# Where a hybrid decoder layer spends its spare wide products: a new deal over the recurrence's chain, the memory's norm and the attention

## The chip, the cores and the metric

The kernel is one program on one core of a Trainium2 chip. Its time is device microseconds (us) of that core, the median of several runs. The engines of the core are TensorE (PE in the profile, PEld for its weight loads), VectorE (DVE), ScalarE (ACT), GpSimd (POOL) and SyncE (SP), which issues nearly all DMA transfers here.

## The reference

One layer of a causal decoder trunk, 1024 tokens of width 1024, in float32. Three branches read the same normalised input `h` through one combined projection `w_in`:

```python
h = rms_norm(x, norm_mix_pre)
z_pool, z_q, z_rwkv, z_gate = split(h @ w_in)     # 512, 512, 3328, 3 x 1024 columns

y_pool = pool_branch(z_pool, ...) @ w_proj_pool   # causal means over 2, 4, 8, 16 tokens, 4 groups

mem_n = rms_norm(mem, mem_norm)                   # 256 memory tokens
k, v  = split(mem_n @ w_mem_kv)                   # 4 heads x 128
y_mem = softmax(q k^T / sqrt(128)) v @ w_proj_mem

zr = z_rwkv + (token_shift(z_rwkv) - z_rwkv) * mu_shift
# RWKV-7: 16 heads of 64, for each token t:
#   sa    = state @ (-kk_t)
#   state = state * w_t + sa (kk_t a_t)^T + v_t k_t^T ;  y_t = state @ r_t
y_rwkv = (groupnorm(y) + bonus) * g @ w_proj_rwkv

gates  = sigmoid(z_gate + gate_b)                 # 3 gates
x = x + rms_norm((gates0*y_pool + gates1*y_rwkv + gates2*y_mem) @ w_o)
x = x + rms_norm(convffn(rms_norm(x)))
```

## The kernel before, in words

**Wide products in triples.** Each float32 operand of a wide product is split into a coarse part and a rest (`hh`, `hl` for the input, `whi`, `wlo` for weights), and `mm3` issues three products 128x512 into one bank: coarse by coarse, coarse by rest, rest by coarse. Three such products are called a triple. The weights come from memory as `wraw` (loads of two k-slices), ScalarE makes `whi` by a cast, GpSimd or VectorE makes `wlo`.

**The recurrence** runs over 16 chunks of 64 tokens. In `chain`, each chunk visits TensorE three times: `pr` (the state and the decayed keys give a right-hand side, copied to `Rs`), `pu` (the inverted triangular matrix, `nt`, times `Rs`, copied to `hv`), and `ph` with `py` (the next state and the output). That makes 48 visits, each waiting for a copy of the one before. The chunks' matrices were written to memory earlier (`d_ar`, `d_nt`, ...) and are loaded by SP two chunks at a time; `nt` lies in the tile that the rows call `pair`. Outputs are normalised with a product `pvar` and stored to `d_y`.

**The filler.** While a visit waits, TensorE is given wide products that nobody needs yet: the projection's blocks of the pool (4), the queries (4) and the gates (24), in the list `fill`. A block is two halves of 512 tokens by eight k-slices, so 16 triples, 512 triples in all. `fill_steps` issues one triple at a time, and when a half is complete, `spilled` evacuates it (ScalarE to `st`, SP to `d_zp`, `d_zq` or `d_zg`). `fill_to(n)` issues triples until n have been issued, and returns the last one. Visit v calls `fill_to(fills(v))` and orders its own first product behind the last triple. A scheduler then orders each engine's instructions by their data and by such hints (`later`).

**The memory and the attention.** Behind the chain, `fill_to(416)` returns `covered`. SP loads the memory (`mraw` from `memT`, eight parts, into room that the chain leaves), ScalarE squares the parts (`msq`, `msqp`), VectorE adds them, and the product `pmm` with a matrix of ones sums over the channels; it is ordered behind `covered`. `mrs` is the reciprocal root of the sum, VectorE multiplies the parts by it, and `mh`, `ml` are the coarse part and the rest. Eight blocks of `w_kv` follow (eight triples each, products of 128x256): four of keys (`kh`, `kl`), four of values, which are transposed (`pvt`, function `turned`) as `vh`, `vl`. Weights of the first two come as `wraw`, of the other six as `kvr` (512 KB, two rooms). Then four heads of attention, each in two halves: scores `psco`, softmax `prb`, transposes `ptr`. Behind each head the products of the pooling and some of the blocks that are left in `fill` (`in_block`) are written.

Of the kernel before, what the change touches and what calls it, by code (L numbers as in the profile page):

```python
# [44 lines left out]
def trunk_kernel(ctx: ExitStack, tc: tile.TileContext, xT, memT, pvec, w_in, w_kv, w_upd, w_upg,  # L45
# [129 lines left out]
    last_mm = [None]  # L175
# [46 lines left out]
    def later(i, ins, plain=False):  # L222

        tc.add_manual_dep(i if plain else i.ins, ins.name, nosync, reason="order")
# [79 lines left out]
    def hrhs(t0):  # L304
        return lambda k: (hh[:, k, t0:t0 + 512], hl[:, k, t0:t0 + 512])
# [35 lines left out]
    def spilled(dst, bias=None):  # L341
        def evac(t0, ps):
            st = wp.tile([P, 512], F32, name="st", tag="st", bufs=3)
            if bias is None:
                spills.append(A.copy(st, ps).ins)
            else:
                A.activation(st, ps, AF.Identity, bias=bias)
            SP.dma_start(dst[:, t0:t0 + 512], st)
        return evac
# [123 lines left out]
    def rwkv_group(g, kv):  # L473
# [183 lines left out]
        if g == 3:  # L657
            w_queue[0] = A
            fill_to(256, solve)
# [186 lines left out]
    fill = [(j, spilled(d_zp[j])) for j in range(4)] + [(4 + j, spilled(d_zq[j])) for j in range(4)]  # L846
    fill += [(34 + j, spilled(d_zg[j], col("gate_b", j))) for j in range(24)]
    filled = []

    def fill_steps(j, evac, behind):  # L850

        ws = load_w(w_in[j], KC, c=1)
        for t0, _ in HALVES:
            ps = psg.tile([P, 512], F32, name="psg", tag="g1")
            rhs = hrhs(t0)
            for k in range(KC):
                m = mm3(ps, ws[k], rhs(k), k == 0, k == KC - 1)
                if k == 0 and behind is not None:
                    later(m, behind)
                filled.append(last_mm[0])  # L860
                if k == KC - 1:
                    evac(t0, ps)
                yield

    current = [iter(())]

    def fill_to(n, behind=None):

        while len(filled) < n:
            if next(current[0], 0) == 0:  # L870
                current[0] = fill_steps(*fill.pop(0), behind)
        return filled[n - 1]

    first_kv = start()
# [4 lines left out]
    hi_on_act[0] = True  # L879
    for g in range(4):  # L880
        kv = rwkv_group(g, kv)
    chain(lambda v: 262 + 138 * v // 47)
    covered = fill_to(416)
    w_queue[0] = SP
    spare[0] = None
    rw_ctx.close()
# [16 lines left out]
    with tc.tile_pool(name="km", bufs=1) as km:  # L903
# [12 lines left out]
        m = PE.matmul(pmm[:, :256], ones, total, start=True, stop=True)  # L916
# [41 lines left out]
        turned(*waiting.pop())  # L958

        lo_on_dve[0] = False  # L960


    pz_ctx = ExitStack()
# [47 lines left out]
    for hd in range(4):  # L1011
        for t0, _ in HALVES:
            s = slice(t0, t0 + 512)
            q = as_.tile([P, 512], F32, name="q", tag="q", bufs=2)
            SP.dma_start(q, d_zq[hd][:, s])
            qh = as_.tile([P, 512], FR, name="qh", tag="qh")
            ql = as_.tile([P, 512], FR, name="ql", tag="ql")
            split(q, qh, ql, V)
            po = pss.tile([P, 512], F32, name="po", tag="s")
            for u in range(2):  # L1020
                ps = psg.tile([P, 2, 256], F32, name="psco", tag="g0")
                for tt in range(2):
                    ts_ = slice((2 * u + tt) * P, (2 * u + tt + 1) * P)
                    mm3(ps[:, tt], (qh[:, ts_], ql[:, ts_]), (kh[:, hd], kl[:, hd]), True, True)
                mx = as_.tile([P, 32], F32, name="mxs", tag="mxs", bufs=2)
                V.reduce_max(mx[:, 0:2], ps, axis=AX.X)
                V.tensor_scalar(mx[:, 2:4], mx[:, 0:2], -SC, None, op0=ALU.mult)
                pr = as_.tile([P, 2, 256], F32, name="prb", tag="prb", bufs=2)
                for tt in range(2):
                    act(pr[:, tt], ps[:, tt], AF.Exp, bias=mx[:, 2 + tt:3 + tt], scale=SC,  # L1030
                        accum_out=mx[:, 4 + tt:5 + tt])
                V.reciprocal(mx[:, 6:8], mx[:, 4:6])
                V.tensor_tensor(pr, pr, mx[:, 6:8].unsqueeze(2).broadcast_to([P, 2, 256]), op=ALU.mult)
                pt = (psc if u else psk).tile([P, 2, 2, P], F32, name="ptr", tag="c" if u else "k")
                for tt in range(2):
                    for m in range(2):
                        PE.transpose(pt[:, m, tt], pr[:, tt, m * P:(m + 1) * P], ident)
                pth = as_.tile([P, 2, 256], FR, name="pth", tag="pth", bufs=2)
                ptl = as_.tile([P, 2, 256], FR, name="ptl", tag="ptl")
                split(pt.rearrange("p m t s -> p m (t s)"), pth, ptl, V)  # L1040
                for m in range(2):
                    mm3(po[:, u * 256:(u + 1) * 256], (vh[:, hd, m], vl[:, hd, m]), (pth[:, m], ptl[:, m]),
                        m == 0, m == 1)
            split(po, oh[hd][:, s], ol[hd][:, s], V)
        pool_products(hd)
        if hd < 2:
            pool_sums(hd + 2)
        for j, ev in fill[hd + min(hd, 2):hd + min(hd, 2) + (2 if hd < 2 else 1)]:
            in_block(j, ev, 1)

    as_ctx.close()
# [794 lines left out]
```

## Time and profile before

| | |
|---|---|
| median of 3 runs | 1961.81 us (1959.63 to 1962.59) |
| profiled execution | 1961.22 us, span 1959.5 us |
| mean granted TensorE clock | 0.997 |
| TensorE busy | 1912.1 us, 98% of the span |
| VectorE, ScalarE, GpSimd busy | 1361.5, 1044.3, 791.9 us |
| from 680 to 696 us (the chain's first two visits): TensorE busy | 13.23 of 16 us |
| from 696 to 889 us (the rest of the chain) | 192.88 of 193 us |
| from 889 to 909 us (to the ones product) | 17.94 of 20 us |
| from 909 to 942 us (norm, keys, values) | 33.00 of 33 us, at a mean clock of 0.96 |
| from 942 to 1030 us (attention) | 84.49 of 88 us |

Times are those of one profiled execution, counted from the span's start. A row of the timeline gives start, duration, engine, line, operation, result and operands, shapes, and how many equal ones it stands for; in brackets, how long the engine had stood idle before it and who released it. `L916` is line 916 of the kernel before. An engine that is busy all the time can still be slow: the granted clock says at what share of its full speed TensorE ran.

### The profile page before, as it was taken

What the parts mean: (1) busy time and instruction counts of PE and PEld (TensorE: products, weight loads), DVE (VectorE), ACT (ScalarE), POOL (GpSimd) and SP (SyncE); (2) the same over time, 40 slices, a digit from 0 to 9 for tenths busy, and PEclk for the clock granted to TensorE, in tenths of its full rate; (3) what the DMA queues carried; (4) which work ended last, traced back from release to release, by engine and by line L of the source; (5) the groups of instructions that cost most, each with busy time, mean ns of one, the idle gap of its engine ahead of it and who ended that gap; (6) DMA issues with size and microseconds to landing.
All of it is one profiled execution on the core that took longest, in us unless ns stands there. A gap on an engine that the chain in (4) does not pass through costs nothing.

```text
span 1959.5 us, 33751 instructions
## 1 busy us (share of the span) xinstructions
PE 1912.1 (98%) x12204; PEld 1543.9 (79%) x12204; DVE 1361.5 (69%) x2022; ACT 1044.3 (53%) x2158; POOL 791.9 (40%) x867
## 2 busy tenths in 40 slices
PE   8999999999999999999999999999999999999997
PEld 6777777777777777777888888888888888888886
DVE  8677567677677435546884443689798888877798
ACT  7685385385384244445665244546554545454544
POOL 4422221321321211111223365565599888822441
PEclk9999999999999999999999999999999999999999
DMA  4325235225239668966318343644322222289775
GB/s 162 129 71 177 96 86 175 90 86 175 94 107 279 190 207 279 300 215 212 108 59 274 123 144 111 225 150 133 122 76 87 81 87 76 97 241 227 172 182 146
DMA packets 269639, 296.26 MB, mean 151 GB/s; under 512 B 18336, under 2 KB 219168, under 8 KB 266400
## 3 DMA queue, kind: packets, MB, share of 16 engines
q1 hardware_dynamic: 248480, 271.56, 43.2%
q0 software_dynamic: 11856, 14.16, 4.4%
q10 hardware_dynamic: 9136, 8.39, 1.4%
q8 instruction: 96, 1.57, 0.3%
q14 instruction: 71, 0.58, 0.1%
HBM read 207.00 MB, written 87.03 MB: 150 GB/s over the span
## 4 chain that ended last, share of the span: by engine, by line
PE 77%; DVE 8%; DMA 6%; ACT 4%; issue 3%; POOL 1%; SPq 0%; ACTq 0%; POOLq 0%; DVEq 0%
PE psg L180 14%; PE psg L182 14%; PE psg L181 14%; PE psf L182 5%; PE psf L180 5%; PE psf L181 5%; PE psd L181 3%; PE psd L182 3%; PE psd L180 3%; PE py L770 2%; DMA wraw<-in_w_in 1%; PE ps L605 1%; DVE tb L651 1%; DVE tb L653 1%; DMA d_bv<-kv 1%
## 5 line engine op out<-in xcount | busy, mean ns | idle before, releaser
L139 POOL TENSOR_TENSOR wlo<-wraw,whi 128x256 fp32r<-128x256 f32 x464 | 410.7, 897 | 833.8 <-ACT whi L132 772.7
L180 PE MATMUL psg<-hh,whi 128*128 128x512 f32 x928 | 380.1, 410 | 12.2 <-ACT whi L132 5.9
L182 PE MATMUL psg<-hh,wlo 128*128 128x512 f32 x928 | 368.0, 397 | 2.7 <-POOL wlo L139 2.2
L181 PE MATMUL psg<-hl,whi 128*128 128x512 f32 x928 | 367.8, 396 | 0.7 <-DVE hl L266 0.6
L132 ACT CAST whi<-wraw 128x256 fp32r<-128x256 f32 x472 | 181.2, 402 | 236.2 <-PE psg L181 99.1
L180 PEld LDWEIGHTS psg<-hh,whi 128*128 128x128 f32 x928 | 175.0, 189 | 60.1 <-ACT whi L132 11.2
L182 PEld LDWEIGHTS psg<-hh,wlo 128*128 128x128 f32 x928 | 175.0, 189 | 44.8 <-POOL wlo L139 7.2
L181 PEld LDWEIGHTS psg<-hl,whi 128*128 128x128 f32 x928 | 175.3, 189 | 40.5 <-issue 4.5
L1172 POOL TENSOR_TENSOR wt<-a,wt 128x256 fp32r<-128x256 f32 x136 | 155.6, 1168 | 35.1 <-ACT wt L1171 35.1
L181 PE MATMUL psd<-f,u 128*128 128x512 f32 x292 | 113.9, 390 | 0.2 <-DVE f L1588 0.2
L180 PE MATMUL psd<-f,u 128*128 128x512 f32 x292 | 113.2, 391 | 0.8 <-ACT f L1584 0.8
L182 PE MATMUL psd<-f,u 128*128 128x512 f32 x292 | 113.7, 389 | 0.0
L182 PE MATMUL psf<-h2h,wt 128*128 128x512 f32 x272 | 105.9, 389 | 0.0
L181 PE MATMUL psf<-h2l,wt 128*128 128x512 f32 x272 | 105.8, 389 | 0.0
L180 PE MATMUL psf<-h2h,wt 128*128 128x512 f32 x272 | 105.8, 389 | 0.0
L1186 DVE SCALAR_TENSOR_TENSOR d<-z,pv,d 128x1023 f32<-128x1023 f32 x68 | 101.2, 1491 | 2.1
L1172 POOL TENSOR_TENSOR wt<-s,wt 128x256 fp32r<-128x256 f32 x68 | 80.0, 1197 | 3.8 <-ACT wt L1171 2.6
L180 PE MATMUL psf<-t,wt 128*128 128x512 f32 x204 | 79.4, 389 | 0.0
L181 PE MATMUL psf<-t,wt 128*128 128x512 f32 x204 | 79.4, 389 | 0.0
L182 PE MATMUL psf<-t,wt 128*128 128x512 f32 x204 | 79.4, 389 | 0.0
L1184 ACT ACTIVATE d<-z,pv 128x1024 f32<-128x1024 f32 x34 | 42.4, 1246 | 65.3 <-DVE z L1266 49.8
L1171 ACT CAST wt<-a 128x256 fp32r<-128x256 f32 x136 | 50.6, 404 | 41.3 <-POOL wt L1172 25.9
(432 smaller groups left out, 4565.7 us busy)
## 6 DMA issues: line engine op xcount, KB each, us to landing
wraw<-in_w_in SPq DMA_DIRECT2D x176, 128.0 KB, 2.3
a<-in_w_fup SPq DMA_DIRECT2D x128, 128.0 KB, 2.3
d_ar<-AR SPq DMA_DIRECT2D x24, 512.0 KB, 3.7
d_zg<-st SPq DMA_DIRECT2D x48, 256.0 KB, 3.7
ring<-d_ar SPq DMA_DIRECT2D x8, 1536.0 KB, 10.5
wraw<-in_w_fup SPq DMA_DIRECT2D x80, 128.0 KB, 2.4
fraw<-d_f SPq DMA_DIRECT2D x33, 256.0 KB, 4.2
d_rb<-RB SPq DMA_DIRECT2D x16, 512.0 KB, 3.9
```

The lines of the kernel that those rows point to most:

```text
L132: i = A.copy(hi, src)
L139: (V if lo_on_dve[0] else G).tensor_tensor(lo, src, hi.bitcast(F32), op=ALU.subtract)
L180: first = PE.matmul(ps, wh, xh, start=start, stop=False)
L181: PE.matmul(ps, wh, xl, start=False, stop=False)
L182: last_mm[0] = PE.matmul(ps, wl, xh, start=False, stop=stop).ins
L605: PE.matmul(ps[:, c], BK[i][up, c0 + c], AR[up, i, 1:3, t], start=True, stop=True)
L651: V.tensor_tensor(tm, X[:, s + 1:, s:s + 1].broadcast_to([P, n, m]), S[:, s:s + 1, 0:m].broadcast_to([P, n, m]), op=ALU.mult)
L770: m = PE.matmul(out_, l, r, **kw)
L1171: A.copy(w[0][:, us], src[u])
L1172: low = eng.tensor_tensor(w[1][:, us], src[u], w[0][:, us].bitcast(F32), op=ALU.subtract)
L1184: A.activation(d, z, AF.Identity, scale=col("cw2", j), bias=col("cb", j))
L1186: V.scalar_tensor_tensor(d[:, n:], z[:, :T - n], col(cw, j), d[:, n:], op0=ALU.mult, op1=ALU.add)
```

## The change

It moves products; it adds none and takes none away.

- The rule that says how many triples are issued by visit v becomes `279 + 121*(v-1)//46` from the second visit on (it was `262 + 138*v//47`); the first visit keeps 262 and the last 400. So 17 triples stand between the first and the second visit, where there were 12.
- `covered`, behind which `pmm` is ordered, is the 424th triple (the end of a half block), where it was the 416th, the end of a block.
- Behind the last `turned`, half a block more (`fill_to(432, ...)`) is issued, ordered behind the values' last product.
- The five blocks left are written behind the heads as 1, 2, 1, 1; it was six, as 2, 2, 1, 1.
- So that a half block may have a hint of its own, `fill_steps` reads it from `tied[0]` when a half begins, instead of taking it when the block begins.

```diff
+    tied = [None]
-    def fill_steps(j, evac, behind):
+    def fill_steps(j, evac):
...
-                if k == 0 and behind is not None:
-                    later(m, behind)
+                if k == 0 and tied[0] is not None:
+                    later(m, tied[0])
...
     def fill_to(n, behind=None):
 
+        tied[0] = behind
         while len(filled) < n:
             if next(current[0], 0) == 0:
-                current[0] = fill_steps(*fill.pop(0), behind)
+                current[0] = fill_steps(*fill.pop(0))
         return filled[n - 1]
...
-    chain(lambda v: 262 + 138 * v // 47)
-    covered = fill_to(416)
+    chain(lambda v: 279 + 121 * (v - 1) // 46 if v else 262)
+    covered = fill_to(424)
...
         turned(*waiting.pop())
 
         lo_on_dve[0] = False
+        fill_to(432, last_mm[0])
...
-        for j, ev in fill[hd + min(hd, 2):hd + min(hd, 2) + (2 if hd < 2 else 1)]:
+        for j, ev in fill[hd + (hd > 1):hd + 1 + (hd > 0)]:
             in_block(j, ev, 1)
```

Where the products stand on TensorE is seen from the order of its instructions. First the chain's second visit, `pu`, before:

```order
L180 MATMUL psg_6746<-hh_146,whi_6723 128x512
L181 MATMUL psg_6746<-hl_147,whi_6723 128x512
L182 MATMUL psg_6746<-hh_146,wlo_6724 128x512
L770 MATMUL pu_6601<-Rs_6520,pair_6519 64x64 x16
L180 MATMUL psg_6746<-hh_146,whi_6729 128x512
```

and now:

```order
L180 MATMUL psg_6663<-hh_146,whi_6652 128x512
L181 MATMUL psg_6663<-hl_147,whi_6652 128x512
L182 MATMUL psg_6663<-hh_146,wlo_6653 128x512
L180 MATMUL psg_6663<-hh_146,whi_6658 128x512
L181 MATMUL psg_6663<-hl_147,whi_6658 128x512
L182 MATMUL psg_6663<-hh_146,wlo_6659 128x512
L770 MATMUL pu_6601<-Rs_6520,pair_6519 64x64 x16
L180 MATMUL psg_6663<-hh_146,whi_6658 128x512
```

Between the first visit and `pu` there are 51 wide products now, 36 before: `pu` comes five triples later in the row. From there to the last visit, the stretches between visits have 121 triples instead of 126, mostly three each in both, with 17 stretches of two now.

Next TensorE at the memory's ones product `pmm` (`msq` are the summed squares), before:

```order
L180 MATMUL psg_9848<-hh_146,whi_9815 128x512
L916 MATMUL pmm_9144<-msq_9145,ones_90 128x256
L181 MATMUL psg_9848<-hl_147,whi_9815 128x512
L182 MATMUL psg_9848<-hh_146,wlo_9816 128x512
L180 MATMUL psg_9900<-hh_146,whi_9877 128x512
L181 MATMUL psg_9900<-hl_147,whi_9877 128x512
```

and now:

```order
L181 MATMUL psg_9132<-hl_147,whi_9127 128x512
L182 MATMUL psg_9132<-hh_146,wlo_9128 128x512
L919 MATMUL pmm_9196<-msq_9197,ones_90 128x256
L180 MATMUL psg_9274<-mh_9224,whi_9251 128x256
L181 MATMUL psg_9274<-ml_9225,whi_9251 128x256
L182 MATMUL psg_9274<-mh_9224,wlo_9252 128x256
```

Ahead of `pmm`, behind the chain's last `pvar`, stand 46 wide products now, 68 before. Behind it the products of the first key block (`mh`, `ml`) follow at once; before there were ten wide products, and 29 more among the keys and values. None is left there now: from the last visit to the values' end, 72 wide products instead of 123.

Last, TensorE at the end of the values, where `pvt` are the transposes, before:

```order
L181 MATMUL psg_9553<-ml_9173,whi_9549 128x256
L182 MATMUL psg_9553<-mh_9172,wlo_9550 128x256
L943 MATMUL pvt_9578<-ident_92,vt_9533 128x128 x2
L180 MATMUL psg_9928<-hh_146,whi_9877 128x512
L181 MATMUL psg_9928<-hl_147,whi_9877 128x512
L182 MATMUL psg_9928<-hh_146,wlo_9878 128x512
L180 MATMUL psg_9928<-hh_146,whi_9883 128x512
L181 MATMUL psg_9928<-hl_147,whi_9883 128x512
L943 MATMUL pvt_9585<-ident_92,vt_9583 128x128 x2
```

and now:

```order
L181 MATMUL psg_9605<-ml_9225,whi_9601 128x256
L182 MATMUL psg_9605<-mh_9224,wlo_9602 128x256
L946 MATMUL pvt_9630<-ident_92,vt_9585 128x128 x2
L180 MATMUL psg_9642<-hh_146,whi_9109 128x512
L181 MATMUL psg_9642<-hl_147,whi_9109 128x512
L182 MATMUL psg_9642<-hh_146,wlo_9110 128x512
L180 MATMUL psg_9642<-hh_146,whi_9109 128x512
L181 MATMUL psg_9642<-hl_147,whi_9109 128x512
L946 MATMUL pvt_9637<-ident_92,vt_9635 128x128 x2
```

The place looks alike, but the products behind the values are now the second half of the block whose first half stands ahead of `pmm`: 24 products and no more, where 21 of a block shared with the keys stood before. What has gone from the memory's stage comes later: 63 wide products between the second and the third head instead of 24, 25 instead of 13 between the third and the fourth. In SP's row, the loads of the pooling (`tz` from `d_zp`), four now and three before, stand right behind the memory's loads, ahead of the values' weights.

## The prediction

> **What bounds the kernel now.** I read the busy shares of the page first, then TensorE's waits, and then the stretch from 680 to 1030 us in order of time, engine by engine.
>
> ```profile
> span 1959.5 us, 33751 instructions
> PE 1912.1 (98%) x12204; PEld 1543.9 (79%) x12204; DVE 1361.5 (69%) x2022; ACT 1044.3 (53%) x2158; POOL 791.9 (40%) x867
> ...
> PE pu L770 <- DMA pair<-d_nt: 2.8, 1, 2.8
> ...
> PE pmm L916 <- issue: 2.1, 1, 2.1
> ```
>
> The page's first rows say that TensorE (PE) is at work 98% of the span: it bounds the kernel, and time is lost only where it stands still or runs slow. The other two are groups of its waits (who waits, for whom, the sum in us, how often, the longest): in the stretch that the change touches, 2.8 us at the chain's second visit (`pu`) and 2.1 us at the memory's ones product (`pmm`). The change adds and removes no product. So the question is where TensorE will stand still afterwards. A wide product starts 0.2275 us after the one before (44 steps from 890.51 to 900.52, rows further down); a triple takes 0.683 us.
>
> **The second visit.** These are rows in order of time from TensorE and of the chain that ended last.
>
> ```profile
> 691.44 0.39 PE L182 MATMUL psg<-hh,wlo 128*128 128x512 f32 x1
> 694.60 1.15 PE L770 MATMUL pu<-Rs,pair 64*64 64x64 f32 x32 [2.77 <-DMA pair<-d_nt]
> 682.66 6.41 DMA d_nt<-NT
> 689.12 5.34 DMA pair<-d_nt
> 690.28 0.41 ACT L132 CAST whi<-wraw 128x256 fp32r<-128x256 f32 x1 [0.95 <-PE psg L181]
> ```
>
> Twelve triples lie between the first visit and the second; the last of their products starts at 691.44 and leaves TensorE at 691.83. Then `pu` waits for its own triangular matrix, written to memory and read back (689.12 + 5.34 = 694.46). Neither transfer depends on a wide product. Five triples more take 15 x 0.2275 = 3.41 us, so `pu` would start near 695.15 instead of 694.60, with 3.41 us of work done meanwhile: **-2.86 us** for all that follows. Their last weights are cast at 690.28 and are needed at 694.4, so they are there. Bounds: 0, if the transfer came later by as much, and -3.4.
>
> **The rest of the chain.** From `pu` to the last visit it has 121 triples instead of 126, five having gone ahead of `pu`: 17 stretches of two triples where before nearly all had three (38 stretches of three before, 29 now, by the order). Its cover is thinnest between `pu` and `ph`:
>
> ```profile
> 866.01 0.58 ACT L808 COPY hv<-pu 64x512 f32<-64x512 f32 x1 [3.67 <-DVE hv L807]
> 867.44 1.15 PE L770 MATMUL ph<-hv,bk 128*64 128x64 f32 x32
> ```
>
> The copy ends at 866.59, `ph` starts 0.85 us later. The new order has two triples instead of three there only where a variance product stands beside them, so I cost this at nothing. If that cover is gone, a place costs at most the missing triple, 0.68 us. SP's loads of the chain are asked for ahead of their use as before.
>
> **Ahead of the ones product.** Rows in order of time, by engine (start, duration), then windows (length, busy time of PE, weight load, DVE, ACT and POOL, the granted clock, the busy share of the DMA engines, GB/s).
>
> ```profile
> 889.31 1.12 PE L714 MATMUL pvar<-Rs,bonesr 128*128 128x512 f32 x2
> 889.87 0.80 PE L182 MATMUL psg<-hh,wlo 128*128 128x512 f32 x1
> 890.51 0.40 PE L180 MATMUL psg<-hh,whi 128*128 128x512 f32 x1
> ...
> 900.52 0.39 PE L182 MATMUL psg<-hh,wlo 128*128 128x512 f32 x1
> ...
> 907.96 1.19 PE L916 MATMUL pmm<-msq,ones 128*128 128x256 f32 x2 [2.06 <-issue]
> 908.59 0.99 PE L181 MATMUL psg<-hl,whi 128*128 128x512 f32 x1
> ...
> 911.45 0.39 PE L181 MATMUL psg<-hl,whi 128*128 128x512 f32 x1
> ...
> 896.03 0.69 DVE L721 TENSOR_TENSOR pair<-pair,gt 128x512 f32<-128x512 f32 x1
> 896.75 0.38 SPq L704 DMA_DIRECT2D d_y<-pair  x1
> 900.07 3.66 SPq L907 DMA_DIRECT2D mraw<-in_memT  x8
> 902.50 0.42 ACT L913 ACTIVATE msq<-mraw 128x256 f32<-128x256 f32 x1 [5.92 <-DMA mraw<-in_memT]
> 906.49 0.75 ACT L913 ACTIVATE msqp<-mraw 128x256 f32<-128x256 f32 x2 [0.43 <-DMA mraw<-in_memT]
> 907.00:909.00 2.00, 1.04 (x3) 0.90 (x4) 0.75 (x2) 0.56 (x2) 0.72 (x1) 0.74 0.25 81
> 909.00:911.00 2.00, 2.00 (x6) 1.61 (x5) 0.58 (x1) 1.77 (x4) 0.74 (x1) 0.50 0.78 215
> 911.00:913.00 2.00, 2.00 (x10) 1.62 (x9) 2.00 (x7) 1.20 (x3) 0.00 (x0) 0.91 0.80 252
> ```
>
> What `pmm` waits for is a path without TensorE: the chain's last output on VectorE (896.03), its store (896.75), the memory's load into the same room (asked for at 900.07), the squares as the load lands (906.49), their sum. That the load waits for the store is read from 900.07 standing 3.3 us behind 896.75. Before, 68 wide products lie between the last `pvar` and `pmm`; now 46. The 46th is done at 900.75. The path loses only the casts between the squares, some 0.3 us, since the load's landing sets the last ones; `pmm` then comes at about 907.65 on the old clock. TensorE stands still 6.8 us there instead of 2.06: **+4.74 us**. Bounds: +3.5 (the path shorter by 1.5, its three squares' casts and one weight load ahead of it) to +5.5.
>
> The clock: after the gap of 2.06 us the windows show 0.74, 0.50 and 0.91 of full speed, and the ten products right behind `pmm` are slow: 908.59 to 911.45 are seven steps in 2.86 us where 1.59 would do. Those ten are gone from there: **-1.3 us**; what runs slow now is the first products of the keys, which wait for VectorE anyway, so I add 0.4 us of the same loss at the place where it bites (0 to 1.7).
>
> The Trainium skill, page "TensorE: Matmul & The Clock Gate", Part 1, says that an idle window of about 3.4 us halves the clock and that about 3.4 us of sustained work brings it back. The halving to 0.50 agrees; that 2.06 us of standing still sufficed does not. By that rule the sum would have 1.7 us in the place of my 0.4.
>
> **From the ones product to the keys.**
>
> ```profile
> 909.19 0.47 ACT L214 ACTIVATE mrs<-pmm,eps 128x256 f32<-128x256 f32 x1 [1.63 <-PE pmm L916]
> 910.41 1.54 DVE L924 SCALAR_TENSOR_TENSOR mraw<-mraw,pv,mrs 128x256 f32<-128x256 f32 x3 [2.56 <-ACT mrs L214]
> 912.37 0.28 PE L180 MATMUL psg<-mh,whi 128*128 128x256 f32 x1
> 917.18 0.42 DVE L125 TENSOR_TENSOR ml<-mraw,mh 128x256 fp32r<-128x256 f32 x1
> 919.69 0.41 ACT L132 CAST whi<-wraw 128x256 fp32r<-128x256 f32 x1 [0.84 <-DMA wraw<-in_w_kv]
> 927.05 0.41 ACT L132 CAST whi<-kvr 128x256 fp32r<-128x256 f32 x1 [1.75 <-DMA kvr<-in_w_kv]
> 935.28 0.28 PE L180 MATMUL psg<-mh,whi 128*128 128x256 f32 x1
> ...
> 937.67 0.28 PE L182 MATMUL psg<-mh,wlo 128*128 128x256 f32 x1
> ...
> 940.88 0.38 PE L943 MATMUL pvt<-ident,vt 128*128 128x128 f32 x2
> ```
>
> Nothing wide is left to cover this. From 909.15, the end of `pmm`, to the first key product (912.37; some 911.25 with one cast fewer ahead of it on ScalarE): **+2.1 us**. Then VectorE makes the eight parts of the normalised memory from 910.41 to 917.60, and the second block's last weights land for a cast at 919.69; the second block ends near 921.0. The two blocks' 48 products, at the 0.1195 us that 935.28 and 937.67, 20 products apart, give, need 5.7 us of the 9.75 us from 911.25: **+4.05 us**. Bounds 2 (the second block's weights a microsecond or two sooner) and 5. The other six blocks need 144 x 0.1195 + 0.5 for the transposes = 17.7 us and are fed by loads of 512 KB that wait for the block two before (the cast at 927.05 waited 1.75 us for one); TensorE was just full there with wide products between, and without them I add **+0.7 us** (0 to 2.5).
>
> So the values end near 921.0 + 17.7 + 0.7 = 939.4 on the old clock, 936.5 on the new one, 4.4 us ahead of 940.88; but 51 wide products fewer are done by then (72 instead of 123 since the last visit), 11.6 us. So it is behind by 11.6 - 4.4 = 7.2 us. The terms so far give the same to 0.2 us: -2.86 + 4.74 - 1.3 + 2.1 + 4.05 + 0.7 = 7.4.
>
> **The attention.** The 51 products run there, half of the first block behind the values, 39 ahead of the third head (63 instead of 24). VectorE has room for it.
>
> ```profile
> 942.00:1023.00 81.00, 77.49 (x440) 63.73 (x438) 71.79 (x132) 51.13 (x134) 23.37 (x23) 1.00 0.26 87
> 947.42 0.39 PE L180 MATMUL psco<-kh,qh 128*128 128x256 f32 x1 [1.07 <-ACT qh L124]
> 995.98 0.39 PE L180 MATMUL psco<-kh,qh 128*128 128x256 f32 x1 [1.12 <-ACT prb L214]
> ```
>
> In this window, from the values to the last head, TensorE is busy 77.49 of 81 us, so more work there is paid for, but for the 3.5 us in which it stands still. The 1.12 us ahead of the third head go under the 39 products. The 1.07 us shrink to 0.3, since 24 products (5.5 us) stand behind the values in the place of 21 and the query still comes 6.5 us behind them (947.42 - 940.88). Of the other 1.3 us I take half. Together 1.12 + 0.77 + 0.65, **-2.5 us** (-3.5 to 0). SP's loads for the pooling, four instead of three, now pass ahead of the values' weights; they do it while TensorE waits for the norm, and cost nothing as long as 2 MB land before 915, which the 215 to 252 GB/s of the windows allow.
>
> The sum is 7.2 + 0.4 - 2.5 = **+5.1 us** on the profiled execution's 1961.22 us (its span of 1959.5 and 1.7 around it): 1966.3. That execution lies 0.6 us below the median of the runs shown, 1961.81; I take about half of that in and forecast **1966.5 us**.
>
> **Rivals.**
> (1) Not slower: the keys' stage, free of wide products, runs at TensorE's own pace. If the parts of the memory and the weights keep up, the 192 products need 192 x 0.1195 + 0.5 = 23.4 us from 911.25 and end at 934.7 on the old clock instead of 939.4; with the attention's waits all gone (0.8 us more) the sum is +5.1 - 4.7 - 0.8 = -0.4 us, 1961 us. For it: VectorE did other things between (it was busy 2.00 of 2 us at 911 to 913, partly with pooling later on), and the loads have 0.80 of the queues' time taken by what now comes earlier. Against it: the 919.69 and 927.05 rows, casts that wait for loads already. It decides if the second block ends before 917.5 on the old clock. With the ones product sooner by 2 us as well it would even be faster, 1958.
> (2) Slower still: the clock stays low through the keys. The gap is three times that which halved it; if it is full again only as the third block starts, the 48 products take 11.4 us at half the pace instead of 5.7, and what VectorE's pace does not hide, with the following block, is 2 to 4 us: 1969. For it: 0.50 in the window behind a gap of 2.06 us. Against it: behind the 2.77 us at `pu` no slow product follows.
> (3) Slower: the chain starves. Five of the 17 places with a triple less losing their 0.68 us give 3.4 us: 1970. Against it: 0.85 us left at the thinnest usual place.
>
> **How the numbers follow.** My own sum 0.52 (it would read 1963.5 to 1968.5), rival 1 0.30, rival 2 0.11, rival 3 0.07. About 0.2%, 3.9 us, is what a measurement of this kernel tells from no change. Slower by more than that: most of the first case (0.40) and rivals 2 and 3 (0.17), 0.57. Within it: the low part of the first (0.12) and most of rival 1 (0.22), 0.34. Faster: rival 1 with an early ones product, 0.09. The range goes from 1961.0 (rival 1) to 1970.5 (rivals 2 and 3 nearly whole).
>
> **What would show it.** After the change `pu` waits for nothing, starts 0.5 us later and has 17 triples ahead. `pmm` shows a wait of 6 to 7 us, the windows behind it a clock of 0.5, and TensorE stands still in pieces of a microsecond until the second block of keys is through. The first scores come some 4 us earlier, and no wait of over 0.5 us is left ahead of the third head. I am wrong if `pmm` waits less than 4 us, or if the keys and values take under 26 us from `pmm`.

## The result, and the profile after

The change made the kernel slower: 1973.68 us (median of 6 runs, 1971.35 to 1980.86) against 1962.16 us (6 runs, 1959.63 to 1966.79), a ratio of 1.0061 with a 95% interval of 1.0041 to 1.0082. That is 11.5 us more, where 4.7 were forecast, and it lies above the upper end of the range, 1970.5 us.

The profiled execution of the changed kernel took 1971.57 us with a span of 1969.9. The first lines of its page:

```profile
span 1969.9 us, 33777 instructions
PE 1913.4 (97%) x12204; PEld 1546.0 (78%) x12204; DVE 1357.4 (69%) x2022; ACT 1045.6 (53%) x2158; POOL 790.5 (40%) x867
```

And groups of its waits on TensorE (who waits, for whom, the sum in us, how often, the longest):

```profile
PE pmm L919 <- DMA tz<-d_zp: 8.1, 1, 8.1
...
PE psg L180 <- ACT mh L124: 2.6, 2, 2.0
...
PE psf L182 <- POOL wt L1176: 1.6, 1, 1.6
PE po L180 <- ACT pth L124: 1.5, 1, 1.5
...
PE psco L182 <- DVE ql L125: 1.2, 1, 1.2
PE psco L180 <- ACT prb L214: 1.1, 1, 1.1
```

TensorE does the same work as before (1913.4 us against 1912.1) in a span that is 10.4 us longer. The wait at `pu` is gone from the list. In its place `pmm` waits 8.1 us, the keys 2.6, and the attention has three waits of over a microsecond, in other places than before.

The stages lie at other times in the two kernels. So I compare windows (length, busy time of PE, weight load, DVE, ACT, POOL, granted clock, DMA share, GB/s) from the last `pvar` to `pmm`, from there to the end of the values, and from there to the attention's output projection. First those of the kernel before:

```profile
889.00:908.00 19.00, 16.94 (x73) 13.16 (x72) 8.74 (x14) 8.70 (x21) 6.17 (x7) 1.00 0.75 229
908.00:941.00 33.00, 33.00 (x229) 30.62 (x230) 25.38 (x61) 18.34 (x52) 1.72 (x3) 0.95 0.61 197
941.00:1033.50 92.50, 88.99 (x499) 73.41 (x498) 77.99 (x139) 59.37 (x147) 25.70 (x26) 1.00 0.27 92
```

and those of the changed kernel:

```profile
884.00:904.00 20.00, 11.90 (x51) 9.10 (x49) 9.06 (x14) 7.67 (x18) 3.85 (x4) 0.87 0.74 235
904.00:936.50 32.50, 28.47 (x200) 26.38 (x201) 24.86 (x61) 16.78 (x49) 0.50 (x1) 0.87 0.45 154
936.50:1040.00 103.50, 99.68 (x551) 83.54 (x550) 78.20 (x139) 62.82 (x153) 29.64 (x30) 1.00 0.28 92
```

Ahead of `pmm` TensorE worked 16.94 of 19 us before and 11.90 of 20 now; from there to the values 33.00 of 33 and 28.47 of 32.5. No other engine is full in these two stages now: this is a stretch in which one thing waits for the next. In the attention TensorE stands still as long as before, 3.8 us against 3.5, in a stage that is 11 us longer. The path ahead of `pmm`, rows in order of time, SP's, ScalarE's and TensorE's:

```profile
892.06 0.38 SPq L704 DMA_DIRECT2D d_y<-pair  x1
892.53 0.53 SPq L348 DMA_DIRECT2D d_zg<-st  x1
895.37 3.18 SPq L910 DMA_DIRECT2D mraw<-in_memT  x7
898.65 0.38 SPq L348 DMA_DIRECT2D d_zg<-st  x1
899.07 0.43 SPq L910 DMA_DIRECT2D mraw<-in_memT  x1
899.54 2.30 SPq L974 DMA_DIRECT2D tz<-d_zp  x4
902.92 0.39 ACT L916 ACTIVATE msqp<-mraw 128x256 f32<-128x256 f32 x1 [1.60 <-DMA mraw<-in_memT]
903.87 0.77 PE L919 MATMUL pmm<-msq,ones 128*128 128x256 f32 x1 [8.10 <-DMA tz<-d_zp]
907.03 0.58 PE L180 MATMUL psg<-mh,whi 128*128 128x256 f32 x1 [1.97 <-ACT mh L124]
```

The store of the last output is asked for at 892.06, the memory's load 3.31 us later, its eighth part at 899.07, behind the store of a filler block. That part is squared only at 902.92, after 1.60 us of waiting for it. The profile names `tz` as what ended `pmm`'s wait, since that came last; what the product reads is `msq`. The four `tz` loads are asked for right behind the eighth part. In the kernel before a store and three loads of weights stood between, and the three `tz` loads came 5 us behind the memory's loads (the text on the change puts them right behind there too):

```profile
905.41 3.31 SPq L168 DMA_DIRECT2D wraw<-in_w_in  x3
908.77 2.21 SPq L970 DMA_DIRECT2D tz<-d_zp  x3
```

The two profiles are single executions, so I set lengths of stages from all traces side by side. Each is the distance between the starts of two instructions: the first `pr`, the last `py`, the last `pvar`, the last product of the values, the first product of the projection behind the attention (`psg<-oh`, the attention's output times `w_proj_mem`; called the output projection here), and the end of the span. The last column but one spans the region in which the change lies. Two traces of the kernel before are of executions longer than its medians (1967.6 and 1970.9 us); the part ahead of the first `pr`, whose instructions stand in the same order in both kernels, took 680.4 to 693.2 us in these six traces and is not in the table.

| kernel (traces) | pr to last py | last pvar to pmm | last pvar to values | values to projection | pr to projection | projection to end |
|---|---|---|---|---|---|---|
| before (first) | 198.0 | 18.7 | 51.5 | 92.5 | 351.0 | 926.2 |
| before (three more) | 198.6, 195.9, 196.0 | 18.3, 18.6, 18.4 | 53.9, 52.1, 51.7 | 92.6, 92.9, 92.8 | 354.2, 349.9, 349.6 | 925.7, 926.4, 926.4 |
| changed (first, again) | 194.8, 194.8 | 19.7, 20.4 | 52.0, 52.6 | 103.4, 103.6 | 359.2, 360.0 | 930.2, 927.5 |

Between the last `pvar` and the values' end the changed kernel has 51 wide products less, 11.6 us at 0.2275, and the stage takes as long as before. (Behind `pmm` there were 29 such products before, the ten that came at once among them; the text on the change counts the ten twice, its 123 against 72 is right.) The products are then done in the attention, which is 10.8 us longer in the mean. The chain gives back 1.1 to 3.8 us. Mean against mean, the part from the first `pr` to the projection is 8.4 us longer (359.6 against 351.2).

### The profile page after: what moved, and what is told of

Its sections match the earlier page's. It is cut to its first block, busy times and chain, and to the rows that moved or that the text cites. A ratio compares the mean times of both kernels' runs of the same rounds, so it can differ in the third digit from the quotient of the medians.

```text
span 1969.9 us, 33777 instructions
## 1 busy us (share of the span) xinstructions
PE 1913.4 (97%) x12204; PEld 1546.0 (78%) x12204; DVE 1357.4 (69%) x2022; ACT 1045.6 (53%) x2158; POOL 790.5 (40%) x867
## 4 chain that ended last, share of the span: by engine, by line
PE 78%; DVE 9%; DMA 5%; ACT 4%; issue 2%; POOL 1%; SPq 0%; POOLq 0%; ACTq 0%; DVEq 0%
PE psg L180 14%; PE psg L182 13%; PE psg L181 13%; PE psf L182 5%; PE psf L181 5%; PE psf L180 5%; PE psd L181 3%; PE psd L180 3%; PE psd L182 3%; PE py L770 2%; DMA wraw<-in_w_in 1%; PE ps L605 1%; DVE tb L651 1%; PE pr L770 1%; DVE tb L653 1%
## 5 line engine op out<-in xcount | busy, mean ns | idle before, releaser
L180 PEld LDWEIGHTS psg<-hh,whi 128*128 128x128 f32 x928 | 174.7, 188 | 60.1 <-ACT whi L132 10.8
```

Of the source, the lines that this page charges most:

```text
L180: first = PE.matmul(ps, wh, xh, start=start, stop=False)
```

## The experiments

**The halves of the change apart, and both kernels once more.** `law_only` has the new rule of the chain and nothing else, `late_only` all else with the old rule.

```diff
law_only (on the kernel before)
-    chain(lambda v: 262 + 138 * v // 47)
+    chain(lambda v: 279 + 121 * (v - 1) // 46 if v else 262)
late_only (on the changed kernel)
-    chain(lambda v: 279 + 121 * (v - 1) // 46 if v else 262)
+    chain(lambda v: 262 + 138 * v // 47)
```

> Only the chain's rule is changed (17 triples ahead of pu, five fewer spread behind it); memory stage and attention as in the kernel before. Theory A (the terms of the prediction stand, the loss lies behind the chain): pu waits for nothing, the last py comes 2.9 to 3.3 us earlier than before counted from the first pr, everything behind keeps its distances, so 2 to 3.3 us faster than before (ratio 0.9983 to 0.999). Rival B (the thinner stretches of the chain cost what pu gains): last py at the same distance as before, 0 to +2 us. Rival C (the late part, the two-layer FFN, lost 4 us in the changed kernel because of the new rule): 1 us slower to 1 us faster with FFN waits of 3 to 4 us.

> Only the other half of the change: 424 instead of 416 ahead of pmm, the half block tied behind the values, blocks 1, 2, 1, 1 in the attention; the chain's old rule. Theory A: the whole loss is here. pu waits 2.8 us as before, pmm waits about 7 to 8 us, the first key products run at a granted clock of 0.5, 11 to 15 us slower than before (the changed kernel's 11.5 plus pu's 2.9, or the 8.2 that the traced region shows plus 2.9). Rival B (the chain's thinner stretches cost): 5 to 8 us slower.

> The changed kernel once more, unaltered, for a second trace and five more times beside the same runs of the kernel before. Theory A (the region from the first pr to the output projection costs 8.2 us, the other 2 to 4 us are scatter of the loads from one execution to the next): the region's distances come out the same to 0.5 us, the FFN's waits differ from the first trace by 1 to 4 us. Rival C (the FFN loses 4 us in every execution of the changed kernel): the same waits of 1.6 us ahead of psf and 0.6 ahead of psn again. 8 to 12 us slower than before.

> The kernel before, unaltered, for a second trace of it. Theory A: the stretch from the first pr to the output projection is 351.0 us long again to 0.5 us, with a wait of 2 us ahead of pmm and 2.8 ahead of pu; the stretches before and behind it scatter by 1 to 3 us. Rival: the waits at pu and pmm are themselves scatter, and come out different by over 1 us.

| | median, us | ratio to before, interval | pr to last py | pr to projection | projection to end |
|---|---|---|---|---|---|
| law_only | 1960.58 (before 1960.80) | 0.9998, 0.9988 to 1.0008 | 194.8 | 348.0 | 929.2 |
| late_only | 1975.67 | 1.0075, 1.0061 to 1.0088 | 199.0 | 362.7 | 927.0 |
| after_again | 1974.70 | 1.0076, 1.0059 to 1.0094 | 194.8 | 360.0 | 927.5 |
| before_again | 1967.64 (one run) | | 198.6 | 354.2 | 925.7 |

The whole loss is in `late_only`, as theory A said (14.9 us slower, 11.5 of them in the region); the thinner stretches of the chain cost nothing (194.8 us in all three traces with the new rule so far). But `law_only` did not bring its 2 to 3 us in the time: its region is 3 us shorter than that of the first trace, the rest 3 us longer. And the second trace of the kernel before shows that its waits are not fixed: 1.9 us at `pu` instead of 2.8 (a little under the 1 us of difference that the rival named; two later traces exceed it), no slow products right behind `pmm`, and keys and values that took 4 us longer from their first product.

**Undo the hint; warm the array; take the norm off the path.** `untied` drops the hint of the half block. `warm` adds 30 products of no use ahead of `pmm`. The two `early` kernels load the memory a second time, early, for the squares and the norm; the later squares, `pmm` and `mrs` are dropped, and the pooling's loads are ordered behind the normalised memory, as in `tz_late` below.

```diff
untied (on the changed kernel)
-        fill_to(432, last_mm[0])
+        fill_to(432)
warm (on the changed kernel)
     covered = fill_to(424)
+    wps = psg.tile([P, 512], F32, name="psw", tag="g1")
+    for n in range(30):
+        m = PE.matmul(wps, hh[:, n % KC, 0:P], hh[:, n % KC, 0:512], start=n == 0, stop=n == 29)
+        later(m, covered)
+        covered = m.ins
early_after (on the changed kernel), early_law (on law_only)
+    mem2 = rw.tile([P, KC, 256], F32, name="mem2", tag="X00")
+    msq2 = rw.tile([P, KC, 256], F32, name="msq2", tag="X02")
+    for k in range(KC):
+        SP.dma_start(mem2[:, k], memT[k * P:(k + 1) * P])
+    ...
+    m = PE.matmul(pmm[:, :256], ones, msq2[:, 0], start=True, stop=True)
+    mrs = wp.tile([P, 256], F32, name="mrs", tag="st", bufs=3)
+    rstd(mrs, pmm[:, :256], 0)
     covered = fill_to(424)
...
```

> The changed kernel with one thing undone: the half block behind the values carries no hint, so that the scheduler may place its products, and those of later blocks, among the keys again (its order does: 69 and 11 wide products around pmm, 26 among the keys). Theory A (the loss is TensorE standing still in the memory's stage for want of wide products): the stretch from the first pr to the output projection is 348 us (before 351.0, the new rule alone 348.05, the changed kernel 359.2 to 360.0), and the time is that of the kernel before to -3 us. Rival B (the loss comes from the blocks' new places in the attention, 1, 2, 1, 1): still 8 us or more slower.

> The changed kernel with 30 products more, of no use to the result, between the 424th triple and pmm: 6.8 us of work in a wait of 8.1 to 8.8 us, so that TensorE is not cold when the keys start. Theory A (the stage waits for the memory's load, norm and weights; the low clock lies under these waits): the clock is 1.00 in the keys, and the end of the keys and values comes 0 to 1 us earlier. Theory B (the granted clock of 0.5 over the first key block is a large part of the loss): 2 to 3.5 us earlier, since the first block's 24 products run in 2.9 us instead of 6.3.

> The changed kernel, with the memory loaded a second time early, into room that the chain's even chunks leave, so that squares, pmm and the reciprocal root are done before the chain's outputs end; the parts to be normalised are loaded as before. Theory A (what pmm waited for was the chain's last store, then the load, then the squares): no wait at pmm, the first key product comes 5 to 7.5 us earlier counted from the last pvar (22.8 us in the changed kernel), and the time is 5 to 7 us below the changed kernel's, 5 to 8 us above the kernel before. Rival (the keys are paced by the loads of their weights, whatever the norm does): the first key is earlier, but the end of the values by less than 3 us.

> The kernel before with the new rule for the chain and with the early norm: wide products lie where the scheduler puts them, in the memory's stage too. Theory A (every wait in this region is a place where TensorE has nothing to do): pu, pmm and the slow products behind pmm give back 2.9 + 2.1 + 1.3 us, the stretch from the first pr to the output projection is 344 to 346 us, the time 3 to 6 us below the kernel before. Rival (what is won ahead of the output projection is lost to the loads behind it, as the new rule alone suggests): the stretch is shorter, the time the same to 1 us.

| | median, us (before 1959.99) | ratio to before, interval | pr to projection | last pvar to values | values to projection |
|---|---|---|---|---|---|
| untied | 1959.77 | 1.0000, 0.9988 to 1.0012 | 348.0 | 51.3 | 92.5 |
| warm | 1973.89 | 1.0077, 1.0056 to 1.0097 | 359.7 | 52.4 | 103.5 |
| early_after | 1964.42 | 1.0026, 1.0015 to 1.0037 | 351.2 | 44.1 | 103.0 |
| early_law | 1964.10 | 1.0018, 1.0007 to 1.0028 | 350.7 | 49.3 | 97.2 |

`untied` is the sharpest: with that one hint gone, the scheduler places wide products among the keys again, the stage is as long as ever (51.3 us) and the loss is gone. `early_after` attacks the same loss from the other end: the products stay where the change put them, but the stage is 8 us shorter, and the region is back at 351.2 us, the mean of the kernel before; the time is still 4.4 us above that of the kernel before, where the changed kernel lay 11.5 and 13.9 us above it: 7 to 9.5 us won, more than A's 5 to 7. Rows of it, the memory's load, VectorE's first normalised part and TensorE's first key:

```profile
894.97 0.38 SPq L704 DMA_DIRECT2D d_y<-pair  x1
895.44 0.53 SPq L348 DMA_DIRECT2D d_zg<-st  x1
898.54 3.18 SPq L923 DMA_DIRECT2D mraw<-in_memT  x7
900.94 1.31 DVE L927 SCALAR_TENSOR_TENSOR mraw<-mraw,pv,mrs 128x256 f32<-128x256 f32 x3 [6.00 <-DMA mraw<-in_memT]
```

The parts still wait for the last output's store (894.97, the load at 898.54), but they are normalised as they land: `pmm` stands 0.96 us behind the last `pvar`, and the first key starts 13.64 us behind `pmm`, so 14.6 us behind the last `pvar` instead of 22.8. So the wait at `pmm` was latency of the path, and where wide products don't cover it, TensorE pays.

`warm` answers less than it was to. Its products end 1.3 us ahead of `pmm`, and the keys start 2.6 us behind it, and the low clock is there after all, only later:

```profile
907.00:909.00 2.00, 0.39 (x1) 0.19 (x1) 1.61 (x5) 1.45 (x4) 0.00 (x0) 1.00 0.90 369
909.00:911.00 2.00, 1.94 (x9) 1.94 (x10) 1.86 (x6) 0.79 (x4) 0.00 (x0) 0.51 0.16 61
911.00:913.00 2.00, 2.00 (x12) 1.90 (x11) 1.94 (x6) 1.04 (x4) 0.00 (x0) 0.64 0.26 51
```

The time did not move, as A said, but B is not refuted by it, since the first block ran at 0.51 here too. What the low clock alone costs in the keys is open. Neither answer of `early_law` came out: its region is hardly shorter than the kernel before's (350.7 us), since the shorter stage (49.3 us against 51.6 of `law_only`) is paid back in the attention, 97.2 us instead of 92.6, where 24 products stand that the stage no longer holds, and the time is above that of the kernel before (ratio 1.0018).

**The loads of the keys' stage, the other direction, and scatter.** `uraw_late` orders the pooling's small weight loads behind the values' weights, `more_434` gives the memory's stage more wide products instead of fewer, and the kernel before was traced twice more.

```diff
uraw_late (on the changed kernel)
-            SP.dma_start(raw, w_kv[j])
+            last_kvr[0] = SP.dma_start(raw, w_kv[j]).ins
...
-        SP.dma_start(raw, ap)
+        i = SP.dma_start(raw, ap)
+        if last_kvr[0] is not None:
+            later(i, last_kvr[0])
more_434 (on untied)
-    covered = fill_to(424)
+    covered = fill_to(434)
...
-        fill_to(432)
+        fill_to(448)
...
-        for j, ev in fill[hd + (hd > 1):hd + 1 + (hd > 0)]:
+        for j, ev in fill[hd:hd + 1]:
```

> The changed kernel with the four small loads of the pooling's weights ordered behind the last load of the values' weights in SP's row. In the changed kernel they stand ahead of the third to sixth of those loads, and the third is issued 5.8 us after the second. Theory A (part of the keys' loss is SP's row: the weights' loads queue behind a load that waits for GpSimd): the third load is issued about 2 us earlier, the two waits of 0.48 and 0.88 us among the keys go, the end of the values comes 1.5 to 2.3 us earlier counted from pmm (32.5 us in the changed kernel). Rival (the loads are paced by their two rooms): the end of the values moves by less than 0.5 us.

> The other direction: the chain's new rule, pmm ordered behind the 434th triple, and one and a half blocks with no hint, so that 108 wide products stand ahead of pmm behind the last pvar (68 before, 46 in the changed kernel) and four blocks are left for the attention. Theory A (wide products are worth most where the memory's path leaves TensorE idle): no wait at pmm, full clock behind it, the stretch from the first pr to the output projection is 343 to 347 us (before 351.0, the new rule alone 348.05), the time 1 to 5 us below the kernel before. Rival (pmm now comes some 7 us late and the keys pay it; the attention lacks the products): 348 us or more, no faster.

> The kernel before, unaltered, one more trace, for a wait in the two-layer FFN ahead of psf (for GpSimd's part of a weight): none in the three traces with the chain's old rule, 0.5 to 2.5 us in all seven with the new one. If the rule brings it: no wait again, and the load of that weight lands 8.4 to 8.6 us after the first psf. If it is scatter: a wait of 0.5 to 2.5 us.

> The same once more, with the same two answers: no wait ahead of psf if the chain's rule brings it, a wait of 0.5 to 2.5 us in one of the two traces if it is scatter. The stretch from the first pr to the output projection shows how far it scatters: 351.0 and 354.2 us so far.

| | median, us (before 1961.49) | ratio to before, interval | pr to projection | pmm to values | values to projection |
|---|---|---|---|---|---|
| uraw_late | 1971.76 | 1.0056, 1.0044 to 1.0069 | 360.1 | 30.8 | 103.4 |
| more_434 | 1959.48 | 0.9989, 0.9979 to 1.0000 | 344.9 | 34.5 | 79.8 |

The changed kernel's loads of the values' weights in SP's row, then those of `uraw_late`:

```profile
910.17 0.33 SPq L934 DMA_DIRECT2D kvr<-in_w_kv  x1
911.97 0.33 SPq L168 DMA_DIRECT2D wraw<-in_w_kv  x1
913.63 0.33 SPq L934 DMA_DIRECT2D kvr<-in_w_kv  x1
914.05 5.82 SPq L368 DMA_DIRECT2D uraw<-in_w_pool  x4
920.31 8.46 SPq L934 DMA_DIRECT2D kvr<-in_w_kv  x4
```

```profile
914.91 0.33 SPq L938 DMA_DIRECT2D kvr<-in_w_kv  x1
916.71 0.33 SPq L168 DMA_DIRECT2D wraw<-in_w_kv  x1
918.37 13.54 SPq L938 DMA_DIRECT2D kvr<-in_w_kv  x5
```

With the small loads out of the way the third load is issued 14.7 us behind `pmm` (16.4 and 16.2 in the two traces of the changed kernel), the two waits are gone, and the end of the values comes 1.4 to 1.6 us earlier behind `pmm` (30.8 against 32.4 and 32.2), at the low end of what A said. But `late_only`, which has the small loads where they were, took 31.3 us, so one trace does not tell how much of this is scatter, and the time, 10.3 us above that of the kernel before, is not clearly below the changed kernel's 11.5 and 13.9. `pmm` itself was late again (20.3 us behind the last `pvar`), and the chain took 1.8 us longer in this trace.

`more_434` goes against the change and has the lowest ratio of the study, 2.0 us below the kernel before with an interval that touches 1. `pmm` comes 26.5 us behind the last `pvar` (18.6 and 18.3 in the two traces of `law_only`), the stage from there to the values is 1.4 to 2.2 us longer, and the attention, with its products gone, is 13 us shorter. So the stage holds 45 wide products more than in the kernel before, 10.2 us at 0.2275, and is 9 to 10 us longer for them: the waits that filler could hide were nearly full before. Its windows to `pmm` and beyond, and the attention:

```profile
885.00:905.00 20.00, 20.00 (x85) 15.53 (x84) 9.53 (x12) 8.09 (x15) 5.09 (x6) 1.00 0.58 179
905.00:945.00 40.00, 37.85 (x231) 32.74 (x229) 25.56 (x60) 21.07 (x58) 5.15 (x8) 1.00 0.64 213
945.00:1030.00 85.00, 82.25 (x484) 68.15 (x483) 76.28 (x144) 54.22 (x145) 21.34 (x21) 1.00 0.24 78
```

The waits at `pu` in the further traces of the kernel before, first `before_again`, then `before_look2`:

```profile
PE pu L770 <- DMA pair<-d_nt: 1.9, 1, 1.9
```

```profile
PE pu L770 <- DMA pair<-d_nt: 0.6, 1, 0.6
```

`before_look3` has 0.8, so the 2.77 us of the first trace were the most of four, with a mean of 1.5. Ahead of `psf` one of the two has no wait and one 0.3 us, both short of the 0.5 us that scatter was to bring; the next experiment comes back to this.

**Two open parts.** `tz_late` orders the pooling's four loads of 512 KB behind the normalised memory; `law_look2` is `law_only` again.

```diff
tz_late (on the changed kernel: what the tz loads are ordered behind)
-            V.scalar_tensor_tensor(mraw[k], mraw[k], col("mem_norm", k), mrs, op0=ALU.mult,
-                                   op1=ALU.mult)
+            mem_read = V.scalar_tensor_tensor(mraw[k], mraw[k], col("mem_norm", k), mrs, op0=ALU.mult,
+                                              op1=ALU.mult).ins
```

> The changed kernel with one hint changed: the four loads of the pooling's sums (tz, 512 KB each) are ordered behind the normalised memory instead of behind pmm's place in the order, so that they no longer follow the memory's eight loads directly in SP's row. Theory A (pmm comes 1.5 us later than reckoned because those 2 MB land at the same time as the memory's last parts): from the last pvar to pmm 18.5 to 19.0 us instead of 19.7 to 20.4. Rival (it is the store of a filler block that stands ahead of the eighth load): 19.7 us or more again. In both, the loads now pass between those of the values' weights, so the end of the values may come later by up to 2 us, and the time is that of the changed kernel to 2 us (11 to 14 us slower than before).

> The chain's new rule alone, one more trace, for what lies behind the attention. From the output projection to the end: 925.7 to 926.4 us in the four traces of the kernel before, 929.2 in the first of this one. If the rule brings the difference: 928 us or more again, with a wait of 0.5 us or more ahead of psf. If it is scatter: 927 us or less. From the first pr to the output projection 348.0 us to 0.3 in either case, since pu waits for nothing.

`tz_late`: 1973.35 us (before 1961.15; ratio 1.0073, 1.0051 to 1.0095), `pmm` 18.9 us behind the last `pvar`. Its SP row and its `pmm`:

```profile
903.51 0.38 SPq L348 DMA_DIRECT2D d_zg<-st  x1
903.93 0.43 SPq L910 DMA_DIRECT2D mraw<-in_memT  x1
907.96 0.77 PE L919 MATMUL pmm<-msq,ones 128*128 128x256 f32 x1 [7.32 <-DVE msq L918]
```

The filler's store still stands ahead of the eighth part, and yet `pmm` is 0.8 to 1.5 us earlier, as A said, so most of the delay goes with the transfers that land with the memory (one trace). The stage as a whole is no shorter for it (51.6 us to the values' end). `law_look2`: 1958.78 us in its one run, 347.1 us from the first `pr` to the projection, 925.7 from there to the end, with no wait at `psf`, so the 929.2 us of `law_only` do not come in every execution. But they are not shown to be mere scatter either. Of the eleven traces of kernels with the new rule, nine have a wait of 0.5 to 2.5 us ahead of `psf`; of the five with the old one none has more than 0.3. From the projection to the end the five take 925.7 to 927.0 us (mean 926.3), the eleven 925.7 to 930.8 (mean 928.2), though in `law_only` TensorE's order there is that of the kernel before. How the rule would reach that far is open. The region of `law_look2` came out 0.9 us shorter than the 348.0 expected, behind the last `pvar`.

## Why the prediction was wrong, point by point

The main mechanism held: without wide products TensorE stands still in the memory's stage, and the products that were moved are paid in the attention. What failed are the gains set against this loss (the waits in the attention, forecast at -2.5 us, where 10.8 of 11.6 us are paid and no wait was saved in sum; the slow products behind `pmm`, -1.3, which most executions do not have), the time of the ones product (1.3 to 2.1 us later than forecast), and the part behind the projection, which the sum put at nothing without a reason and which came out 2.6 us longer.

- **`pu`** (-2.86): the mechanism is right; in every trace of the new rule `pu` starts 12.9 us behind `pr`, with five triples more done. But the price was one execution's. With the mean wait of 1.5 us the term is about -1.6; the distance from `pr` to the last `py` shrank by 2.4 us in the mean.
- **The rest of the chain** (nothing): right, as the same distance shows.
- **The ones product** (+4.74, from a path 0.3 us shorter): wrong by 1.3 to 2.1 us. The path is 1.0 to 1.7 us longer. The failed step is the sentence that the pooling's four loads "cost nothing": they land with the memory's last parts (`tz_late` takes them away and gets 18.9 us, still some 0.5 us above the forecast 18.3).
- **The slow products** (-1.3): again one execution. In the other three traces of the kernel before, a wait of 1.7 to 2.0 us at `pmm` left the clock at full speed, so there was mostly nothing to gain (the last section shows what decides). A row of one of them, the two microseconds from `pmm`:

```profile
908.30:910.30 2.00, 2.00 (x9) 1.70 (x10) 0.21 (x1) 1.33 (x4) 0.84 (x2) 1.00 0.32 91
```

- **From the ones product to the end of the values**: forecast at 31.8 us (907.65 to 939.4), measured at 32.4 and 32.2. Right in kind: TensorE stands still there in pieces, from the load's landing and the weights. Taking the three points together, the stage behind the last `pvar` was forecast to shrink from 51.5 to 50.1 us (50.5 with the 0.4 of cold clock) and did not shrink at all. Rival 1, a stage at TensorE's own pace, would have taken some 27 us (907.65 to 934.7) and did not come.
- **The attention** (-2.5): a gain that did not come. The 51 products were to cover waits there, but TensorE's waits sum to 3.8 us now against 3.5, and 10.8 of the products' 11.6 us are paid. The wait of 1.12 us ahead of the third head went as forecast. The 1.07 us ahead of the first scores only moved: 1.2 us for `ql`, four products further on. Two new waits stand in the second head, 1.1 us for `prb` and 1.5 for `pth`. All three lie inside a head, between its first scores and its outputs, and the 63 products between the second and the third head do nothing for them.
- **Behind the attention** (not in the sum): 927.5 and 930.2 us in the two traces of the changed kernel, 925.7 to 926.4 in four of the kernel before. As said above, a part of this goes with the new rule of the chain, by a path that no run shows. The times say the same in another way: in each of the eleven comparisons of medians the time is 1.4 to 5.4 us worse than the region's length alone would make it (in `law_only`, for one, the region is 3.1 us shorter than the mean of 351.2 and the time only 0.2). Part of that may come from the yardstick, four single executions of the kernel before; the rest stays open.

Put together in the table's terms, mean of the four traces before against mean of the two after: to the last `py` -2.4 us (forecast -2.9), from the last `pvar` to the values 0.0 (forecast -1.0, with the cold clock), from there to the projection +10.8 (forecast 11.6 - 2.5 = +9.1). That is 8.4 us in the region, where the prediction had some 5.2; `late_only` and `untied` bear out that this loss lies in the moved products. Another 2.6 us lie behind the projection (forecast nothing). So about half of the miss is in the sizes of the terms inside the region, and the other half in a part that the forecast held constant, whose cause is open.

## What to carry to other kernels

A stage that is bound by a chain of latencies takes as long with filler as without it, up to what its waits can hold. Up to there filler is free, and where TensorE is busy anyway it is paid: taking 51 products out of such a stage cost 10.8 of their 11.6 us, while 45 more of them than before made the same stage 9 to 10 us longer (`more_434`). Ask of each wait that is to be covered where in the row it stands: work put down in one piece between two heads covers none of the waits inside them. And price a wait from several executions: the two gains of this forecast ahead of the attention were the largest of four traces.

## What the runs showed of the hardware

A wait of about the same length leaves TensorE's clock low in one execution and full in the next. At `pmm` the granted clock fell to 0.50 behind waits of 2.06 us (first trace of the kernel before), 2.01 (`law_only`) and 2.06 (`untied`). It stayed at 1.00 behind 1.73, 2.00 and 1.81 us in the other three traces of the kernel before and 1.70 in `law_look2`, and also behind the 2.77 us at `pu` in the first trace.

The traces show what decides. In each of the 16, the instants at which the granted clock changes between 1.00 and 0.50 lie whole multiples of 3.413 us apart, to 0.01 us. Here are windows between such instants, first of the kernel before (`pu`, then `pmm`), then of `before_look2` (`pmm`):

```profile
689.51:692.92 3.41, 2.32 (x11) 1.58 (x9) 0.38 (x1) 0.99 (x2) 1.42 (x2) 1.00 0.72 247
692.92:696.34 3.42, 1.74 (x35) 1.61 (x36) 0.56 (x1) 0.00 (x0) 0.00 (x0) 1.00 0.59 225
904.54:907.96 3.42, 1.36 (x7) 0.81 (x6) 2.37 (x6) 2.47 (x8) 1.79 (x3) 1.00 0.57 193
907.96:911.37 3.41, 3.41 (x8) 2.75 (x9) 0.95 (x2) 1.94 (x5) 1.14 (x2) 0.50 0.59 178
```

```profile
903.08:906.49 3.41, 3.18 (x15) 2.29 (x13) 1.69 (x4) 2.96 (x9) 1.17 (x2) 1.00 0.85 265
906.49:909.91 3.42, 1.65 (x7) 1.43 (x8) 1.26 (x3) 2.18 (x7) 1.11 (x3) 1.00 0.35 102
909.91:913.32 3.41, 3.30 (x19) 2.36 (x17) 3.23 (x8) 2.44 (x7) 0.64 (x1) 1.00 0.61 212
```

The 2.06 us at `pmm` lie in one window, of which TensorE works 1.36 us, and the next window runs at 0.50. The 2.77 us at `pu` are divided by the end of a window, and so are the 2.00 us of `before_look2`; no window there stands still for more than 1.77 us, and the clock stays. Over all traces, from 620 to 1100 us, every window at full clock in which TensorE stood still for 1.91 us or more is followed by a fall (14 of them), and of those with up to 1.82 us one only (`warm`, 1.64 us). So a gap matters by how much of it falls into one window, and where the windows begin differs from execution to execution.

The Trainium skill, page "TensorE: Matmul & The Clock Gate", Part 1, says that the activity window runs freely, so that the number of cold products differs from run to run; these traces agree with that, while its idle window of about 3.4 us is more than what sufficed here. In the changed kernel, whose wait was 8.1 us, TensorE stopped at 895.8 us, the clock fell to 0.50 at 898.8, and it was back at 1.00 at 912.4, four windows later and 5.4 us after the first key product.
